# GpSimd's store of one output group: three transfers become eight, with other shares for the DMA engines

## The chip, the core and the metric

The kernel runs on one core of a Trainium2 chip. The metric is the device time of one execution in microseconds (us); of several executions the median counts. Three executions before the change took 516.02, 516.07 and 517.08 us, so the median is 516.07 us.

The core has five instruction queues: PE (TensorE), DVE (VectorE), ACT (ScalarE), POOL (GpSimd) and SP (SyncE), and sixteen DMA engines that carry every load and every store.

## The reference

The reference is a batched matrix product in float32, 128 products of a 256x512 by a 512x384 matrix:

```python
b1, b2, m, k, n = 8, 16, 256, 512, 384
x       # (8, 16, 256, 512) float32
weight  # (8, 16, 512, 384) float32
np.matmul(x, weight).astype(np.float32)
```

Every input is read once (64 MiB of `x`, 96 MiB of `weight`) and every output is written once (48 MiB).

## The kernel before

The 128 products are taken in `NG = 32` groups of `G = 4`. One group needs 2 MiB of `x` (tile `x_sb`, two buffers), 3 MiB of weights (`w_sb`, two buffers) and makes 1.5 MiB of output (`out_sb`, four slots of eight rows per partition). Input arrives as float32; DVE and ACT cast it to bfloat16 (`cast_x`, `cast_w`, `cast_short`), PE transposes `x` (`transpose`), ACT brings the transposes from PSUM to SBUF (`evacuate`), PE multiplies (`multiply`, for the last group `multiply_full`), and ACT copies the products from PSUM to `out_sb` (`copy_out`).

Every load and nearly every store is issued by SP in an order written out by hand (`on_sync`, line 312): the loads of the first four groups; then a loop over 26 groups that issues the load of `x` of group n+4, the store of group n and the load of the weights of group n+4; then the loads of groups 30 and 31, and at the end the stores of groups 27 to 31. The first four and the last two groups load their weights in two halves (`is_short`). The last group uses another layout (`is_full`): its load of `x` and its store move shorter runs.

One store is missing from SP's order: that of group 26, the sixth last (`SHARED = NG - 2 - LAG`, line 62). GpSimd issues it in `store_rest` (line 164), the only thing it does after building an identity matrix at the start. It waits until ACT has copied group 26 out and until the store of group 25 has landed. A store of a group covers 128 partitions with 12288 bytes each (eight rows of 384 float32). Before the change it goes in three transfers of 5, 120 and 3 partitions. An instruction that resets the cursor from which GpSimd's transfers are dealt to the DMA engines (`inc_swdge_sem` with `reset_dge_cursor`) stands ahead of the first and of the third. Each transfer adds 16 to `rest_out`.

`rest_out` is waited for in one place: ACT's `copy_out` (line 292) writes group 30 into the slot of `out_sb` that group 26 used, so ahead of its first copy of group 30 ACT waits for `16 * 3`.

At the end SP waits for the stores of groups 28 to 30 (`o_end`, line 329), runs sixteen increments of a semaphore that nobody reads (lines 330 to 333), and waits for the store of group 31 (`o_fin`, line 334), which ends the program.

Of the kernel before, what the change touches and what calls it, by code (L numbers as in the profile page):

```python
# [12 lines left out]
def kernel(  # L13
# [10 lines left out]
    _, _, _, N = weight.shape  # L24
# [18 lines left out]
    R = G * M // P  # L43
    T = R // 2
    SH, SL = 2, 4
    NG = B // G
# [5 lines left out]
    LAG = 4  # L52
# [6 lines left out]

    PAD = 12  # L60

    SHARED = NG - 2 - LAG

    ctx.enter_context(tc.tile_critical(sync_engine=mybir.EngineType.Pool, no_gpsimd_drain=True))  # L64

    def sbuf(name, shape, dtype, n):
        return [
            ctx.enter_context(nc.sbuf_tensor(f"{name}{s}", shape, dtype)) for s in range(n)
        ]
# [6 lines left out]
    def sems(name, n):  # L76
        return [tc.alloc_semaphore(f"{name}{s}") for s in range(n)]
# [9 lines left out]
    out_sb = sbuf("out_sb", [P, OS * R, N], fp32, 1)[0]  # L87
# [16 lines left out]
    rest_out = sems("rest_out", 1)[0]  # L104
# [59 lines left out]
    def store_rest(e):  # L164
        n = SHARED
        e.wait_ge(o_copied, n * T + T + BIAS)
        e.wait_ge(o_out[(n - 1) % 2], 16 + 16 * ((n + 1) // 2))
        dram = o_rows[n * G * M : (n + 1) * G * M].rearrange("(p r) n -> p r n", r=R)
        a = slot(0, NG, n) * R
        p = 0  # L170
        for k, reset in ((5, True), (120, False), (3, True)):
            if reset:
                e.inc_swdge_sem([], [], mode="reset_dge_cursor")
            e.dma_start(  # L174
                out=dram[p : p + k],
                in_=out_sb[p : p + k, a : a + R],
                max_dma_last_dim=R // 2 * N * 4,
            ).then_inc(rest_out, 16)
            p += k

    def is_shared(n):
        return isinstance(n, int) and n == SHARED

    def slot(t, U, s):
        return (t * U + s) % OS
# [106 lines left out]
    def copy_out(e, t, U, s, q):  # L292
        n = t * U + s
        if q == 0:
            if isinstance(n, int) and is_shared(n - OS):
                e.wait_ge(rest_out, 16 * 3)
            elif not isinstance(n, int) or n >= OS:
                e.wait_ge(o_out[s % 2], (t * (U // 2) + s // 2) * 16 + (16 - OS // 2 * 16 + 16))
        e.wait_ge(p_made, n * T + (q + 1 + BIAS))
        e.copy(  # L300
            out=out_sb[:, bass.ds(slot(t, U, s) * R + 2 * q, 2), :],
            in_=po[(s * T + q) % PO][:, :, :N],
        ).then_inc(o_copied, 1)

    def on_gpsimd(e):
        e.memset(identity[:], 0.0).then_inc(id_done, 1)  # L306
        e.wait_ge(id_done, 1)
        make_identity(nc, identity[:], nomemset=True)
        e.drain().then_inc(id_done, 1)
        store_rest(e)  # L310
# [70 lines left out]
    def on_scalar(e):  # L381
# [8 lines left out]
        def step(t, U, s):  # L390
            short = is_short(t * U + s + 1)
            evacuate(e, t, U, s + 1, range(T - 1))
            for q in range(T):
                copy_out(e, t, U, s, q)
                if q == 0:
                    evacuate(e, t, U, s + 1, range(T - 1, T))
                if q == 0 and short:
                    e.sem_inc(w_acast, CA)
                if q > 0 and not short:
                    last = CA if q == T - 1 else q  # L400
                    cast_w(e, t, U, s + 1, range(CV + q - 1, CV + last), q == 1)
# [11 lines left out]
        for q in range(T):  # L413
            copy_out(e, 0, NG, NG - 1, q)
# [36 lines left out]
```

## Time and profile before

| | |
|---|---|
| median of three executions | 516.07 us |
| the profiled execution's own time | 515.93 us |
| its span in the profile | 514.2 us |
| read and written in HBM | 167.77 MB and 50.33 MB |
| mean rate over the span | 424 GB/s |
| DVE and ACT busy | 397.6 us (77%) and 409.6 us (80%) |
| PE busy | 312.7 us (61%) |
| POOL busy | 3.8 us (1%) |
| granted TensorE clock, mean | 0.792 |

The profile shows one execution. Its first part gives the busy time of each engine, its second the span in 40 equal slices, its third the DMA queues, where q1 is what SP issues and q0 what GpSimd issues. The fourth part follows the chain of work that ended last, the fifth lists the costliest groups of instructions, the sixth the DMA issues with the time from issue to landing. "Busy" for the DMA engines is the time that their packets took, as a share of sixteen engines. The trace behind the profile also holds each DMA packet with its queue, its size, its start and its length, though not the number of the engine that moved it.

### The profile page before, as it was taken

How to read it: one execution, taken by the hardware profiler on the slowest of the kernel's cores; microseconds unless marked ns; L12 is line 12 of the kernel's file. 1: busy time of each engine (PE TensorE's matmuls, PEld its weight loads, DVE VectorE, ACT ScalarE, POOL GpSimd, SP SyncE). 2: the span in 40 equal slices, each digit the busy share in tenths (PEclk: the TensorE clock that was granted, in tenths of full speed). 3: DMA queues.
4: the chain of work that ended last, by engine and by line, in shares of the span. 5: the costliest groups of instructions: out<-in, count | busy, mean ns of one | idle time of the engine just before them, and what ended most of it. 6: DMA issues, size and time to landing. Idle time of an engine off the chain costs nothing.

```text
span 514.2 us, 11663 instructions
## 1 busy us (share of the span) xinstructions
PE 312.7 (61%) x4512; PEld 220.0 (43%) x4512; DVE 397.6 (77%) x462; ACT 409.6 (80%) x387; POOL 3.8 (1%) x9
## 2 busy tenths in 40 slices
PE   2276737546575656865666754577547576655872
PEld 2254425434354443543444543445434354442551
DVE  2788757797777887778977779777798777887980
ACT  1365577897987997898989799879897987998662
POOL 0000000000000000000000000000000000010000
PEclk9698878777876887686778687878777886878697
DMA  8999999999999999999999999999999999999997
GB/s 335 430 427 422 441 422 425 432 431 437 428 422 434 432 431 435 423 428 433 437 429 433 422 434 434 431 432 422 433 437 434 429 427 429 431 436 421 422 429 306
DMA packets 15686, 218.18 MB, mean 424 GB/s; under 512 B 1728, under 2 KB 1728, under 8 KB 3008
## 3 DMA queue, kind: packets, MB, share of 16 engines
q1 hardware_dynamic: 15312, 216.54, 98.8%
q0 software_dynamic: 368, 1.57, 0.7%
q8 instruction: 3, 0.05, 0.0%
q14 instruction: 3, 0.02, 0.0%
HBM read 167.77 MB, written 50.33 MB: 424 GB/s over the span
## 4 chain that ended last, share of the span: by engine, by line
DMA 55%; DVE 31%; issue 9%; PE 1%; DVEq 1%; SPq 1%; ACT 0%; POOLq 0%
DMA w_sb<-in_weight_dram 55%; DVE w_bf L207 20%; DVE w_bf L223 5%; DVE x_bf L194 5%; PE po L283 1%; SPq L138 0%; DVEq L358 0%; SPq L121 0%; DVEq L64 0%; DVEq L203 0%; ACT out_sb L300 0%; SPq L133 0%; DVEq L191 0%; DVEq L217 0%; SPq L446 0%
## 5 line engine op out<-in xcount | busy, mean ns | idle before, releaser
L207 DVE CAST w_bf<-w_sb 32x1536 bf16<-32x1536 f32 x286 | 271.9, 951 | 81.7 <-DMA w_sb<-in_weight_dram 70.5
L265 PE MATMUL po<-w_bf,x_t 128*32 128x384 bf16 x3968 | 194.6, 355 | 35.2 <-DVE w_bf L207 23.3
L247 PE MATMUL pt<-identity,x_bf 128*128 128x128 f32 x512 | 113.1, 409 | 155.2 <-DVE x_bf L194 155.2
L207 ACT CAST w_bf<-w_sb 32x1536 bf16<-32x1536 f32 x130 | 190.9, 1468 | 5.1 <-DMA w_sb<-in_weight_dram 2.0
L247 PEld LDWEIGHTS pt<-identity,x_bf 128*128 128x128 f32 x512 | 101.6, 223 | 167.5 <-issue 167.0
L265 PEld LDWEIGHTS po<-w_bf,x_t 128*32 128x32 bf16 x3968 | 115.4, 104 | 112.9 <-issue 50.0
L300 ACT COPY out_sb<-po 128x768 f32 (+1 forms) x128 | 102.4, 800 | 59.3 <-PE po L265 54.1
L234 ACT COPY x_t<-pt 128x1024 bf16<-128x1024 bf16 x128 | 123.5, 1020 | 20.6 <-PE pt L247 20.0
L194 DVE CAST x_bf<-x_sb 128x1024 bf16<-128x1024 f32 x128 | 80.0, 688 | 12.4 <-DMA x_sb<-in_x_dram 11.6
L223 DVE CAST w_bf<-w_sb 64x1536 bf16<-64x1536 f32 x48 | 45.8, 955 | 7.3 <-DMA w_sb<-in_weight_dram 6.0
L234 ACT ACT_TABLE_LOAD x1 | 1.3, 1283 | 10.8 <-PE pt L247 10.8
L174 POOL DMA_DIRECT2D out_dram<-out_sb x3 | 3.1, 1040 | 458.7 <-DMA out_dram<-out_sb 458.7
L283 PE MATMUL po<-w_bf,x_t 128*128 128x384 bf16 x32 | 5.4, 326 | 1.6 <-DVE w_bf L223 1.6
L283 PEld LDWEIGHTS po<-w_bf,x_t 128*128 128x128 bf16 x32 | 3.1, 98 | 3.9 <-issue 1.9
masks.py:199 POOL TENSOR_SCALAR_AFFINE_SELECT identity<-identity 128x128 f32<-128x128 f32 x1 | 0.3, 284 | 0.2 <-POOL identity L306 0.2
L306 POOL MEMSET identity<- 128x128 f32 x1 | 0.2, 205 | 0.5 <-POOLq L64 0.5
L435 POOL MEMSET const-bfloat16-1.0<- 128x1 bf16 x1 | 0.1, 97 | 0.0
L435 POOL MEMSET const-uint8-127<- 128x1 uint8 x1 | 0.1, 97 | 0.0
L435 POOL MEMSET const-float32-0.0<- 128x1 f32 x1 | 0.1, 93 | 0.3 <-issue 0.3
L435 POOL MEMSET const-float32-1.0<- 128x1 f32 x1 | 0.1, 93 | 0.0
## 6 DMA issues: line engine op xcount, KB each, us to landing
w_sb<-in_weight_dram SPq DMA_DIRECT2D x26, 3072.0 KB, 18.1
x_sb<-in_x_dram SPq DMA_DIRECT2D x32, 2048.0 KB, 22.2
out_dram<-out_sb SPq DMA_DIRECT2D x31, 1536.0 KB, 24.9
w_sb<-in_weight_dram SPq DMA_DIRECT2D x12, 1536.0 KB, 16.7
out_dram<-out_sb POOLq DMA_DIRECT2D x1, 1440.0 KB, 17.0
out_dram<-out_sb POOLq DMA_DIRECT2D x1, 60.0 KB, 7.3
out_dram<-out_sb POOLq DMA_DIRECT2D x1, 36.0 KB, 17.9
```

The costliest lines, as they stand in the source:

```text
L174: e.dma_start(out=dram[p : p + k], in_=out_sb[p : p + k, a : a + R], max_dma_last_dim=R // 2 * N * 4,).then_inc(rest_out, 16)
L194: e.tensor_copy(out=x_bf[s % BS][:, rows].rearrange("p r (s q c) -> p r s q c", s=S, c=KO), in_=x_sb[s % XS][:, rows].rearrange("p r (q s ...
L207: copy(out=w_bf[(s * G + i) % WBS][h * C : (h + 1) * C], in_=w_sb[s % WS][i * C : (i + 1) * C, h * KO : (h + 1) * KO, :],).then_inc(w_vcas ...
L223: e.tensor_copy(out=w_bf[(n * G + d * SH + a) % WBS][h * p : (h + 1) * p], in_=w_sb[n % WS][a * p : (a + 1) * p, r : r + KO, :],).then_inc ...
L234: e.copy(out=x_t[s % TS][:, 2 * q : 2 * q + 2], in_=pt[(s * T + q) % PT][:].bitcast(bf16),).then_inc(t_copied, 1)
L247: ins = e.transpose(pt[(s * T + q) % PT][:, rr, h, :], words[:, 2 * q + rr, h :: KO // 2], identity[:],)
L265: ins = e.matmul(po[(s * T + q) % PO][mine, rr, :N], x_t[s % TS][:, 2 * q + rr, ko // 2, mine, ko % 2], w_bf[(s * G + i) % WBS][:, ko, :], ...
L283: ins = e.matmul(po[(s * T + q) % PO][:, rr, :N], x_t[s % TS][:, 2 * q + rr, ko // 2, :, ko % 2], w_bf[(s * G + q) % WBS][:, ko, :], start ...
L300: e.copy(out=out_sb[:, bass.ds(slot(t, U, s) * R + 2 * q, 2), :], in_=po[(s * T + q) % PO][:, :, :N],).then_inc(o_copied, 1)
L306: e.memset(identity[:], 0.0).then_inc(id_done, 1)
L435: nc = _bacc.Bacc("TRN2", target_bir_lowering=False, num_devices=1)
```

## The change

`store_rest` sends group 26 in eight transfers instead of three. The list gives for each whether the cursor is reset ahead of it, its first partition, the count of partitions, and which of the eight rows of each partition it takes (`lo` to `hi`). The first five partitions go in two halves of four rows, as transfers one and four. The rest goes whole, in transfers of 3, 72, 40, 2, 4 and 2 partitions. The cursor is reset four times. The longest run of one descriptor, `max_dma_last_dim`, stays half of what a partition sends in that transfer: 6144 bytes, and 3072 in the two half transfers. ACT waits for `16 * 8` in place of `16 * 3`. Bytes, source, destination and the waits ahead of the store are as before, and nothing else in the program differs.

```diff
-    SHARED = NG - 2 - LAG
+    SHARED, PARTS = NG - 2 - LAG, 8
...
-        p = 0
-        for k, reset in ((5, True), (120, False), (3, True)):
+        H = R // 2
+        parts = [
+            (True, 0, 5, 0, H),
+            (False, 5, 3, 0, R),
+            (False, 8, 72, 0, R),
+            (True, 0, 5, H, R),
+            (False, 80, 40, 0, R),
+            (False, 120, 2, 0, R),
+            (True, 122, 4, 0, R),
+            (True, 126, 2, 0, R),
+        ]
+        assert len(parts) == PARTS
+        for reset, p, k, lo, hi in parts:
             if reset:
                 e.inc_swdge_sem([], [], mode="reset_dge_cursor")
             e.dma_start(
-                out=dram[p : p + k],
-                in_=out_sb[p : p + k, a : a + R],
-                max_dma_last_dim=R // 2 * N * 4,
+                out=dram[p : p + k, lo:hi],
+                in_=out_sb[p : p + k, a + lo : a + hi],
+                max_dma_last_dim=(hi - lo) // 2 * N * 4,
             ).then_inc(rest_out, 16)
-            p += k
...
             if isinstance(n, int) and is_shared(n - OS):
-                e.wait_ge(rest_out, 16 * 3)
+                e.wait_ge(rest_out, 16 * PARTS)
```

## The prediction, made before the changed kernel ran

> **What bounds the kernel now.** The head of the page first, then its DMA queues and the chain that ended last.
>
> ```profile
> span 514.2 us, 11663 instructions
> ...
> DMA  8999999999999999999999999999999999999997
> DMA packets 15686, 218.18 MB, mean 424 GB/s; under 512 B 1728, under 2 KB 1728, under 8 KB 3008
> ...
> q1 hardware_dynamic: 15312, 216.54, 98.8%
> q0 software_dynamic: 368, 1.57, 0.7%
> q8 instruction: 3, 0.05, 0.0%
> q14 instruction: 3, 0.02, 0.0%
> ...
> DMA 55%; DVE 31%; issue 9%; PE 1%; DVEq 1%; SPq 1%; ACT 0%; POOLq 0%
> ```
>
> The sixteen DMA engines are full from the first slice to the last but one: 98.8% + 0.7% of their time. No byte is saved by this change, so only the ends can give time: engines that stop early while others still work. The windows of the last 7 us show that. The two columns that matter stand at the end of each row, DMA share and GB/s.
>
> ```profile
> 505.50:506.00 0.50, 0.00 (x0) 0.00 (x0) 0.00 (x0) 0.00 (x0) 0.00 (x0) 1.00 0.86 369
> 506.00:506.50 0.50, 0.00 (x0) 0.00 (x0) 0.00 (x0) 0.00 (x0) 0.00 (x0) 1.00 0.70 295
> 506.50:510.00 3.50, 0.00 (x0) 0.00 (x0) 0.00 (x0) 0.00 (x0) 0.00 (x0) 0.79 1.01 406
> 510.00:510.40 0.40, 0.00 (x0) 0.00 (x0) 0.00 (x0) 0.00 (x0) 0.00 (x0) 0.50 1.01 399
> 510.40:511.00 0.60, 0.00 (x0) 0.00 (x0) 0.00 (x0) 0.00 (x0) 0.00 (x0) 0.50 0.50 200
> 511.00:511.50 0.50, 0.00 (x0) 0.00 (x0) 0.00 (x0) 0.00 (x0) 0.00 (x0) 0.50 0.31 123
> 511.50:512.00 0.50, 0.00 (x0) 0.00 (x0) 0.00 (x0) 0.00 (x0) 0.00 (x0) 0.50 0.27 102
> 512.00:512.50 0.50, 0.00 (x0) 0.00 (x0) 0.00 (x0) 0.00 (x0) 0.00 (x0) 0.50 0.06 25
> ...
> SPq L330 <- DMA out_dram<-out_sb: 3.0, 1, 3.0
> SPq L333 <- DMA out_dram<-out_sb: 1.3, 1, 1.3
> ```
>
> At 510.4 half of the engines are done; four or five work on to 512.0. What is done after 510.4 is 0.6 x 0.50 + 0.5 x (0.31 + 0.27 + 0.06) = 0.62 us of all sixteen. Spread evenly it would end at 511.0 instead of about 512.3: **1.3 us is the most that levelling can give**, and the dip to 0.70 ahead of 506.5, engines that wait for the last store, adds at most 0.2 us. SP waits for the stores to the end (3.0 and 1.3 us), so the last landing sets the time. Arithmetic is not behind it:
>
> ```profile
> 481.78 24.11 SPq L160 DMA_DIRECT2D out_dram<-out_sb  x5
> ...
> 499.28 5.37 PE po L283 x32
> ...
> 504.67 0.80 ACT out_sb L300
> ```
>
> The last store is issued at 505.5, as soon as ACT has copied; by the packet records early engines start it at 506.44 and end it at 510.4, late ones take it up when the stores ahead of it are done.
>
> **Who is late.** No view names the DMA engine of a packet, but the trace's packet records can be strung together: each packet begins some 4 ns before the recorded end of the one before it on its engine, and every engine moves the same list of SP's packets. That gives sixteen strings. Lag below is how far an engine ends a store behind the earliest engine (us), after the store of group 25 (just ahead of GpSimd's) and of group 30; "full" counts 6144-byte packets of q0. Strings are named by the start of their first packet (ns).
>
> ```
> first packet  1949 1955 1977 1998 2008 2056 2122 2209 2376 2469 2664 2775 2789 2942 2981 3418
> lag, group 25 0.00 1.12 1.24 0.93 0.20 0.13 0.62 3.56 0.25 0.47 0.67 0.48 2.50 2.49 2.60 0.91
> full packets    16   18   20   20   16   16   16    2   20   16   16   16   16   16   16   16
> lag, group 30 0.00 1.59 2.14 1.84 0.19 0.13 0.63 1.48 1.16 0.48 0.66 0.47 2.54 2.50 2.62 0.90
> ```
>
> So GpSimd's store is already a lever: one engine gets one partition (two packets) and falls from last to the middle; two partitions more cost 0.91 us (1.84 - 0.93), or 0.455 each. The row of q0 in the stretch in which it runs agrees: 23.7% of 16 engines x 16 us over 128 partitions is 0.474.
>
> ```profile
> q0 software_dynamic: 365, 1.57, 23.7%
> ...
> out_dram<-out_sb POOLq DMA_DIRECT2D x1, 1440.0 KB, 17.0
> out_dram<-out_sb POOLq DMA_DIRECT2D x1, 60.0 KB, 7.3
> out_dram<-out_sb POOLq DMA_DIRECT2D x1, 36.0 KB, 17.9
> ```
>
> Three engines remain 2.5 to 2.6 late. Early in the run each lost about a microsecond to one of q8's three packets (instructions), at 15.2, 39.3 and 46.0 us; these are the rows of q8 in three windows of 0.5 us, from 15.0, 39.0 and 45.8 (13% of sixteen engines x 0.5 us is 1.04 us of one engine):
>
> ```profile
> q8 instruction: 1, 0.02, 12.9%
> ...
> q8 instruction: 1, 0.02, 13.8%
> ...
> q8 instruction: 1, 0.02, 13.6%
> ```
>
> **How the parts are dealt.** q0's 368 packets are 16 x (3 + 17 + 3): in each transfer every engine gets as many entries as a carrying engine (two per partition, plus one for the semaphore), idle ones as 4-byte fillers. So 5 partitions went to five engines, 120 to fifteen by eights, 3 to three; 120 began behind the five, and skipped the fifth. I count places from the cursor's reset. By the same dealing the new list gives: halves, places 0 to 4; 3 to places 5 to 7; 72 on twelve by sixes, 8 to 15 and 0 to 3; after a reset, the other halves on 0 to 4; 40 on ten by fours, 5 to 14; 2 to places 15 and 0; 4 to 0 to 3; 2 to 0 and 1. Partitions by place, before and after:
>
> ```
> place    0  1  2  3  4  5  6  7  8-14  15
> before  10 10 10  9  1  8  8  8     8   8
> after   10  9  8  8  1  5  5  5    10   7
> ```
>
> The strings with 20, 18 and 2 full packets are places 0 to 2, 3 and 4. The other eleven, three of them late, are places 5 to 15 in an order that the trace doesn't tell outright.
>
> The Trainium skill, DMA: Bandwidth & Descriptors, section "Why a DMA increments its semaphore by 16 and not by 1", has the count of engines as the largest number up to 16 that divides the partitions, but names an exception on this path with sixteen engines and partitions / 16 rounded up. The 368 packets fit the first; whether 72 and 40 keep to it no row shows. By the exception the sum would be that of rival three.
>
> **The sum.** If the late three hold places 5 to 7, each gives up three partitions: 2.62 - 1.37 = 1.25. Seven of the eight early ones take two more: 0.66 becomes 1.57, and 0.90 becomes 1.81, or 0.44 if that one is place 15. Places 0 to 2 keep 2.14 at worst (if the engine with 2.14 is place 0), 1.39 at best (1.84 loses one partition, 2.14 loses two: 1.23). Place 3: 1.13; place 4 stays at 1.48. The worst lag is thus 1.57 to 2.14 instead of 2.62: a gain of 1.05 down to 0.48. I take the upper end, because the string with 0.90 began last of all, which points to place 15, and only one order in three leaves 2.14 where it is.
>
> Costs. Entries per engine go from 23 to 16-fold (3+3+13+3+9+3+3+3) = 640 packets, 40 each. Seventeen more of 9 ns, half of it overlapped: 0.08 us for each engine, on the path. POOL's issues:
>
> ```profile
> 460.46 3.12 POOL L174 DMA_DIRECT2D out_dram<-out_sb  x3 [458.75 <-DMA out_dram<-out_sb]
> ...
> 493.66 0.80 ACT L300 COPY out_sb<-po 128x768 f32<-128x768 f32 x1 [0.39 <-PE po L265]
> ```
>
> Eight instead of three at 1.04 us is 8.3 us, to 468.8; nothing is queued behind them on POOL, so nothing is paid. The resets pay at most as much as an issue, and have the same cover. The wait for `16 * 8`: the old store had landed by 480.5 (the last issue at 462.6 plus 17.9). One turn of q0 per engine took (480.5 - 465) / 23 = 0.67 us, as q1's packet goes in between; forty turns end by 492 at most, sooner where group 31's short load packets alternate. ACT's first copy of group 30 stands at 493.66, and what is queued behind it is the rest of group 30 and then 31. The cover is 1.7 us or more; if it were gone, ACT's delay would have to pass the slack of the last store, 506.44 against the late engines' 508.5, before it cost.
>
> So -1.05 + 0.08 = -0.97. The profiled execution took 515.93, its span 514.2 with 1.7 around it, and stands 0.14 under the median: 514.96 from the one, 515.10 from the other. I forecast **515.0 us**.
>
> **Rivals.** (1) The late three hold places 8 to 14. They then get two partitions more: 2.62 + 0.91 = 3.53, so +0.91 + 0.08, 517.1 us; slower. It decides as soon as one of them is there. For it: in order of first packets they are the 13th to 15th. Against it: that order puts the fifth place 8th, or 14th, since 2209 and 2942 end the first load in the same ns and may be swapped; with the second reading the fifth place stands right among the late three, as 5 to 7 would. (2) The lateness moves between executions: one of three took 1.0 us longer (517.08), the size of one q8 packet. Then gains and losses mix, about 516.0. Against it: the other two executions and the profiled one lie within 0.14. (3) 72 and 40 are dealt over all engines, by fives and threes: the fifth place gets 9 instead of 1, 1.48 + 8 x 0.455 = 5.1, +2.5, 518.6 us. (4) The lateness that is levelled is refilled, for example since the last store can't start before 506.44 or instructions are fetched late by other engines: half the gain at most, 515.6.
>
> **Numbers.** No change is within 0.2%, 1.03 us, or 515.04 to 517.10, about what measurement can tell. The forecast has 0.60 and straddles that line (514.8 to 515.6): 0.38 faster, 0.22 no change. Rival 1 has 0.20 (0.14 slower, 0.06 none), rival 2 0.07 (0.02, 0.02, 0.03 slower), rival 3 0.08, all slower, rival 4 0.05, none. Faster 0.40, same 0.35, slower 0.25. The range, 514.6 to 517.1, holds all but rival 3 and the far half of rival 1; its low end is the profiled 515.93 less the 1.3 of full levelling.
>
> **What would show it.** Dealing: q0 with 640 packets and 1.57 MB, 1990 packets under 512 B. Places: in the last windows the DMA share stays near 1 to about 511 and is gone by 511.5; if rival 1 holds, three engines work on to 513.2 (a share near 0.19); if rival 3, one engine alone to 515. Span 513.2. The waits on POOL and ACT: eight issues from 460.5 to 469, ACT's copy of group 30 at 493.7, still released by PE. A share that falls at 510.4 as before would mean that the last 2 us have another cause than the dealing.

## The result, and the profile after

The changed kernel takes **517.32 us** (median of 11 executions, 517.19 to 517.50) where the kernel before takes 515.95 in the same comparison (515.68 to 517.08): a ratio of 1.0026, with a 95% interval of 1.0018 to 1.0033. It is 1.37 us slower, where 1 us faster was forecast. The head of the page of the changed kernel, its DMA queues, GpSimd's group of issues, and the size and landing time of those transfers:

```profile
span 515.5 us, 11670 instructions
...
DMA packets 15926, 218.19 MB, mean 423 GB/s; under 512 B 1968, under 2 KB 1968, under 8 KB 3248
...
q1 hardware_dynamic: 15312, 216.54, 98.6%
q0 software_dynamic: 608, 1.57, 0.8%
...
L185 POOL DMA_DIRECT2D out_dram<-out_sb x8 | 6.4, 805 | 458.8 <-DMA out_dram<-out_sb 458.8
...
out_dram<-out_sb POOLq DMA_DIRECT2D x1, 864.0 KB, 13.9
out_dram<-out_sb POOLq DMA_DIRECT2D x1, 480.0 KB, 15.7
out_dram<-out_sb POOLq DMA_DIRECT2D x2, 30.0 KB, 10.4
```

The bytes are the same, and the span grew by 1.3 us. q0's 608 packets are 16 x 38. The windows of the last 8 us of the changed kernel (DMA share and GB/s at the end of each row):

```profile
506.00:506.50 0.50, 0.00 (x0) 0.00 (x0) 0.00 (x0) 0.00 (x0) 0.00 (x0) 1.00 0.63 270
506.50:510.00 3.50, 0.00 (x0) 0.00 (x0) 0.00 (x0) 0.00 (x0) 0.00 (x0) 0.61 0.96 387
510.00:510.40 0.40, 0.00 (x0) 0.00 (x0) 0.00 (x0) 0.00 (x0) 0.00 (x0) 0.50 1.03 407
510.40:511.00 0.60, 0.00 (x0) 0.00 (x0) 0.00 (x0) 0.00 (x0) 0.00 (x0) 0.50 0.83 328
511.00:511.50 0.50, 0.00 (x0) 0.00 (x0) 0.00 (x0) 0.00 (x0) 0.00 (x0) 0.50 0.26 104
511.50:512.00 0.50, 0.00 (x0) 0.00 (x0) 0.00 (x0) 0.00 (x0) 0.00 (x0) 0.50 0.18 74
512.00:512.50 0.50, 0.00 (x0) 0.00 (x0) 0.00 (x0) 0.00 (x0) 0.00 (x0) 0.50 0.20 80
512.50:513.00 0.50, 0.00 (x0) 0.00 (x0) 0.00 (x0) 0.00 (x0) 0.00 (x0) 0.50 0.21 84
513.00:513.50 0.50, 0.00 (x0) 0.00 (x0) 0.00 (x0) 0.00 (x0) 0.00 (x0) 0.50 0.02 6
```

From 511.5 to 513.0 the share stands at 0.18 to 0.21. One engine of sixteen is 0.0625, so three engines work alone for 1.5 us: the mark that the first rival had set for itself. By the trace's semaphore records the last store lands at 513.57, where it landed at 512.69 before: +0.88. The other 0.4 us lies behind the landing, a stretch that the prediction had left out. These are the drains of GpSimd's sequencer in the block that ends the program, by their line (least / median / greatest ns), before and after:

```profile
L446 POOLq DRAIN  x3: 34/108/313, 513.0 to 513.9; - x3
```

```profile
L456 POOLq DRAIN  x3: 34/108/722, 513.9 to 515.2; - x3
```

The longest one comes first, right after SP's last wait, and the program ends behind it: 0.722 - 0.313 = 0.41 us. 0.88 + 0.41 is the 1.3 us of the span.

The packet records of the changed kernel, strung together as for the prediction, and ordered by their full packets (one more string with twenty, which is place 0, and those of places 1 to 3 are left out; none of them is late):

```
full packets  lag after store 25 -> lag after store 30
20, places 8-14   2.24 -> 3.95   2.42 -> 4.15   2.51 -> 4.21   (the late three)
20, places 8-14   0.16 -> 1.84   0.23 -> 1.93   0.30 -> 1.98   0.71 -> 2.39
10, places 5-7    0.00 -> 0.06   0.06 -> 0.15   0.53 -> 0.00
14, place 15      0.82 -> 1.13
 2, place 4       3.54 -> 2.18
```

The three engines with ten packets, which gave up three partitions each, were early ones; the late three have twenty. They end their last store at 512.87 to 513.07, where the late three of the kernel before ended theirs at 512.12 to 512.24. (Lag counts from the earliest engine. That is now one of those that gave up partitions, so all the others read some 0.8 us more than in the table before.)

### The profile page after: what moved, and what is told of

Read it like the earlier page. It is cut to its first block, busy times and chain, and to the rows that moved or that the text cites. A ratio compares the mean times of both kernels' runs of the same rounds, so it can differ in the third digit from the quotient of the medians.

```text
span 515.5 us, 11670 instructions
## 1 busy us (share of the span) xinstructions
PE 311.7 (60%) x4512; PEld 220.8 (43%) x4512; DVE 397.7 (77%) x462; ACT 409.6 (79%) x387; POOL 7.1 (1%) x14
## 4 chain that ended last, share of the span: by engine, by line
DMA 55%; DVE 31%; issue 9%; PE 2%; SPq 0%; DVEq 0%; ACT 0%; POOLq 0%
DMA w_sb<-in_weight_dram 55%; DVE w_bf L217 22%; DVE x_bf L204 5%; DVE w_bf L233 3%; PE po L293 1%; PE po L275 1%; SPq L138 0%; DVEq L201 0%; DVEq L64 0%; ACT out_sb L310 0%; SPq L133 0%; SPq L121 0%; DVEq L227 0%; SPq L456 0%; POOLq L64 0%
## 5 line engine op out<-in xcount | busy, mean ns | idle before, releaser
L185 POOL DMA_DIRECT2D out_dram<-out_sb x8 | 6.4, 805 | 458.8 <-DMA out_dram<-out_sb 458.8
```

What stands on the lines that cost most here:

```text
L185: e.dma_start(out=dram[p : p + k, lo:hi], in_=out_sb[p : p + k, a + lo : a + hi], max_dma_last_dim=(hi - lo) // 2 * N * 4,).then_inc(rest_ ...
```

## The experiments

The times of the kernel before beside these runs were 515.91 (e1 to e4), 515.85 (e5 to e8), 515.80 (e9 to e11, one execution), 515.95 (e12), 516.00 (e13, e14) and 515.96 (e15, e16). Each kernel starts from the changed one, unless it says otherwise; only the list of transfers is shown (reset, first partition, partitions, first and last row), and the limit on a run where it differs.

**Which places are late (e1).** Fifteen transfers of 15, 14, ... 2 and at last 9 partitions, each after a reset, so that each place has its own number of packets.

```diff
+            (True, 0, 15, 0, R),
+            (True, 15, 14, 0, R),
+            (True, 29, 13, 0, R),
...
+            (True, 117, 2, 0, R),
+            (True, 119, 9, 0, R),
```

> The share of each place is made different, so that each DMA engine's string of packets tells its place: fifteen transfers of 15, 14, ... 2 and 9 partitions, a reset ahead of each, give places 0 to 15 the counts 15, 15, 14, 13, 12, 11, 10, 9, 8, 6, 5, 4, 3, 2, 1, 0. Theory (the three engines that lose a microsecond to q8's instruction packets hold places 8 to 14, and the time went to their two further partitions): all three strings with a q8 packet show counts from 8 down to 1. Rival (they sit elsewhere, or move from run to run, and the time went into the number of transfers): one of them at least shows 9 or more, or 0. The time itself is no test here; POOL's last DRAIN, if it goes with the number of transfers, is 0.31 + 12 x 0.082 = 1.3 us.

521.53 us in one execution. The strings that are 2.89, 2.31 and 2.27 late after store 25 carry six, four and two full packets, thus three, two and one partition: **places 12, 13 and 14**. The slow engine, 3.64 late, has the 24 packets of place 4. So the first rival's condition holds in this execution, and holds for all three; the changed kernel's own strings, with twenty packets on each of its late three, agree. The end of GpSimd's drain also followed the number of transfers, 15 here:

```profile
L463 POOLq DRAIN  x3: 34/107/1293, 517.2 to 519.1; - x3
```

**The number of transfers, apart from the shares (e2, e5).** Eight transfers, but the shares of before. The 120 partitions go in two halves of four rows. In e2 the limit on a run of memory is 6144 bytes, so that each such half is one run; in e5 it stays at 3072 bytes, so that each half has two runs by the instruction (in both traces a half moves as one packet of 6144 bytes).

```diff
             (True, 0, 5, 0, H),
+            (False, 5, 120, 0, H),
             (True, 0, 5, H, R),
+            (False, 5, 120, H, R),
+            (True, 125, 3, 0, 2),
+            (True, 125, 3, 2, 4),
+            (True, 125, 3, 4, 6),
+            (True, 125, 3, 6, 8),
...
-                max_dma_last_dim=(hi - lo) // 2 * N * 4,
+                max_dma_last_dim=min(hi - lo, H) * N * 4,
```

The last two lines are e2's alone.

> Eight transfers as in the changed kernel, but every place gets the partitions that it had before (10, 10, 10, 9, 1, then 8). Theory (0.9 us of the 1.3 us in the spans are the two further partitions on the late engines, 0.4 us is POOL's last DRAIN, which grows by 0.08 us with each transfer): +0.4 to +0.5 us over the kernel before, DRAIN near 0.72 us, last landing as before near 512.7. Rival A (the number of transfers is the whole price): +1.3 us. Rival B (the shares are the whole price): 0.

> The second experiment again, now with two runs of a descriptor per partition, as the change has them, so that the 120 partitions go to fifteen engines behind the first five and the slow engine of place 4 gets one partition, as before the change. Eight transfers, old shares. Theory (0.9 us of shares on the late engines, 0.4 us of POOL's last DRAIN): last landing as before (512.7), DRAIN 0.72 us, +0.4 to +0.5 us over the kernel before. Rival A (the number of transfers is the whole price): +1.3 us. Rival B (shares alone): 0.

e2 missed what it was made for: 518.93 us (518.87 to 519.05), a ratio of 1.0059 [1.0045, 1.0073]. Its last windows show one engine alone (a share of 0.06) from 512.0 on; its packets end near 514.5:

```profile
511.50:512.00 0.50, 0.00 (x0) 0.00 (x0) 0.00 (x0) 0.00 (x0) 0.00 (x0) 0.50 0.29 111
512.00:512.50 0.50, 0.00 (x0) 0.00 (x0) 0.00 (x0) 0.00 (x0) 0.00 (x0) 0.50 0.06 25
...
513.00:513.50 0.50, 0.00 (x0) 0.00 (x0) 0.00 (x0) 0.00 (x0) 0.00 (x0) 0.50 0.06 25
```

By the strings it is the slow engine: the 120 partitions were dealt by eights over places 0 to 14, both times, and gave place 4 nine partitions instead of one; the engine of place 15 got none. The last store lands at 515.23 instead of 512.69: +2.5, the price that the third rival had put on such a dealing. Nearly all the rest of e2's +3.0 us is GpSimd's drain (714 ns instead of 313). With two runs in each partition (e5) the same 120 began behind the five and skipped place 4, as in the kernel before. The Trainium skill, DMA: Bandwidth & Descriptors, section "Why a DMA increments its semaphore by 16 and not by 1", knows both ways of dealing: the largest divisor up to 16, and for some direct copies sixteen engines with partitions / 16 rounded up, from engine 0. e2 looks like the second (120 / 16 rounded up is 8), the others like the first; here the number of runs in a partition decided which, since the limit on a run is all in which e2 and e5 differ.

e5: 516.29 us (516.02 to 516.82), +0.44 against 515.85, a ratio of 1.0008 [0.9999, 1.0017], with the old shares confirmed by the strings, the last landing at 512.87 (512.69 before) and this drain:

```profile
L456 POOLq DRAIN  x3: 34/107/722, 513.2 to 514.5; - x3
```

By the times alone +0.44 is not clear of noise; the drain's part of it stands in the trace, 0.722 - 0.313 = 0.41. Between the two profiled spans the five transfers more cost 0.6 us: the drain, and 0.18 on the landing.

**The drain taken out of the end (e3, e4).** The changed kernel (e3) and the kernel before (e4), with GpSimd draining as soon as its store has landed, 30 us ahead of the end:

```diff
         store_rest(e)
+        e.wait_ge(rest_out, 16 * PARTS)
+        e.drain()
```

> The changed kernel, with GpSimd waiting for its own store and draining at once, some 20 us ahead of the end, where it has nothing else to do. Theory (POOL's last DRAIN retires the transfers and is on the path after the last landing): the last DRAIN falls from 0.72 to 0.1 us or so, the time by 0.5 to 0.6 us against the changed kernel, to +0.8 us over the kernel before. Rival (the DRAIN is long for another reason, as the last landing): the last DRAIN stays near 0.72 us and the time with it.

> The kernel before, with the same early drain after its three transfers. Theory: the last DRAIN falls from 0.31 to 0.1 us or so, and the time by 0.2 us, which would make it the fastest so far. Rival: no change in either.

```profile
L322 POOLq DRAIN  x1: 722/722/722, 484.2 to 484.2; - x1
...
L458 POOLq DRAIN  x3: 34/34/108, 514.0 to 514.6; - x3
```

Those are e3's drains: the 722 ns are now at 484.2, and the last drains take 34 to 108 ns. e3: 516.65 us (516.38 to 517.13), ratio 1.0016 [1.0007, 1.0025], 0.67 less than the changed kernel. e4: 515.75 (515.56 to 515.87), ratio 0.9996 [0.9987, 1.0005], 0.16 less than the kernel beside it. With the drain out of both, the shares make 516.65 - 515.75 = 0.90 us (with whatever else eight transfers cost besides the drain, which e5 leaves small). So the 1.37 us fall into 0.90 for the shares (e3 against e4) and 0.44 for the number of transfers (e5 against before): 1.34.

**Fewer partitions where the lateness is (e6, e7, e8).** The idea of the change with the places that e1 found. e6 gives places 12 to 14 five partitions, 0 to 3 ten, 4 one and the others nine; e7 gives 12 to 14 four, 5 to 11 ten, 0 to 3 nine, 15 eight and 4 one (the last partition is spread over all engines, with a shorter limit on its run); both with the early drain. e8 is e7 without it.

```diff
             (True, 0, 5, 0, H),
-            (False, 5, 3, 0, R),
-            (False, 8, 72, 0, R),
+            (False, 5, 45, 0, R),
             (True, 0, 5, H, R),
-            (False, 80, 40, 0, R),
-            (False, 120, 2, 0, R),
-            (True, 122, 4, 0, R),
-            (True, 126, 2, 0, R),
+            (False, 50, 49, 0, R),
+            (False, 99, 3, 0, R),
+            (False, 102, 25, 0, R),
+            (False, 127, 1, 0, R),
...
-                max_dma_last_dim=(hi - lo) // 2 * N * 4,
+                max_dma_last_dim=(hi - lo) // (2 if k > 1 else R) * N * 4,
```

That is e7; e6 has 60, then 35, 3 and 25, and the old limit.

> Places 12 to 14, where the staircase run found the three late engines, get five partitions; places 0 to 3 ten, 4 one, 5 to 11 and 15 nine; six transfers, early drain. Theory: the late engines fall below 1.5, and the largest lag after the store of group 30 becomes that of places 1 and 3 (about 2.0, two engines that each lost a microsecond to an instruction packet of q14 and now have ten), instead of 2.6: -0.55 us, and -0.2 us for the DRAIN: 515.1 to 515.2 us where the kernel before takes 515.9. Rival (the shares of this store don't reach the end, and the changed kernel lost its time to something else): no faster than the kernel before with the early drain, 515.75.

> Shares cut to the lags that the staircase run shows: places 12 to 14 four, 5 to 11 ten, 0 to 3 nine, 4 one, 15 eight, and one partition spread over all sixteen; seven transfers, early drain. Theory: the largest lag after the store of group 30 is 1.5 to 1.7 instead of 2.6, -0.9 us, and -0.2 us for the DRAIN: 514.8 us. Rival (as in the run before): 515.75.

> The same shares and transfers without the early drain. Theory: last DRAIN 0.31 + 4 x 0.082 = 0.64 us, last landing as in the run before, so 0.6 us slower than that one: 515.4 us. Rival (the DRAIN is no part of the path): as the run before.

The profiled executions of e6 and e7 came out as worked out, within 0.2: 515.31 and 514.90 us. e8's, 515.84, is 0.4 above what was expected: its drain took 640 ns as worked out, but its last store landed 0.41 later than e7's (512.26 against 511.85). e7's last windows have no tail left:

```profile
510.40:511.00 0.60, 0.00 (x0) 0.00 (x0) 0.00 (x0) 0.00 (x0) 0.00 (x0) 0.50 0.49 195
511.00:511.50 0.50, 0.00 (x0) 0.00 (x0) 0.00 (x0) 0.00 (x0) 0.00 (x0) 0.50 0.15 59
511.50:512.00 0.50, 0.00 (x0) 0.00 (x0) 0.00 (x0) 0.00 (x0) 0.00 (x0) 0.50 0.00 0
```

The medians did not: 515.87 (515.31 to 516.31), 516.39 (514.88 to 516.76) and 516.91 (515.84 to 517.63), ratios of 1.0000 [0.9991, 1.0009], 1.0002 [0.9993, 1.0011] and 1.0021 [1.0012, 1.0030]. e7 has two groups of times: four executions from 514.88 to 515.11, seven from 516.38 to 516.76, and nothing between. The changed kernel has no such groups, nor has the kernel before, which was above 516.5 in one execution only (517.08). (Where the times fall into two groups, the ratio given is not that of the medians: e7's median lies 0.54 above the 515.85 beside it, at a ratio of 1.0002.)

**What makes the second group (e9 to e16).** e9, e10 and e11 are e7 again, to catch a profile of the upper group.

> The same kernel as e7_late_four_rest_nine_ten, looked at again, to catch an execution of its second group of times (516.4 to 516.8 against 514.9 to 515.1). Theory: lateness is not the same in every execution (the second of the rivals), so in an execution near 516.4 the largest lag of an engine at store 30 is about 1.5 us above the 1.64 of the first profile, at a place that the first profile had level, and the last landing is near 513.35 where it was 511.85. Rival a: the landing stays within 0.3 us of 511.85 and the 1.5 us lie behind it, in the last DRAIN. Rival b: the whole chain before the last store (ACT's copies of group 30) is later by 1.5 us, and the lags are as they were.

> A third look at the same kernel. By the theory a time near 514.9 goes with a last landing near 511.85 and a time near 516.4 with one near 513.35 and a largest lag near 3.1 us; by rival a the landing is the same in both, by rival b the issue of the last store is later by the difference.

> A fourth look at the same kernel, with the expectations of the third: theory, time 516.4 with a largest lag near 3.1 us at store 30; rival a, the same landing with a longer end; rival b, a later last store with the same lags.

They took 515.22, 515.22 and 515.25 us, all near the lower group, so they told nothing of the upper one. In the profiles of e7, e9 and e10 the late three lie in places 12 to 14; e11 took the same time.

e12 gives all of places 10 to 15 six partitions, e13 all of 8 to 14 seven (and place 4 four), e14 gives places 5 to 10 five.

```diff
             (True, 0, 5, 0, H),
+            (False, 5, 75, 0, R),
             (True, 0, 5, H, R),
+            (False, 80, 10, 0, R),
+            (False, 90, 27, 0, R),
+            (False, 117, 11, 0, R),
```

That is e13; e12 has 75, then 25 and 6, four times 4 after a reset, and 1; e14 has 45, then 6, 63, 8 and 1.

> Places 0 to 3 get ten partitions, 4 one, 5 to 9 ten, and all of 10 to 15 six (one partition is spread over all), with the early drain. Theory: the late three do not hold places 12 to 14 in every execution but a neighbouring three in most (11 to 13 or 13 to 15), and that made the second group of e7_late_four_rest_nine_ten: an engine that is 2.5 late and has ten partitions where it was to have four ends 6 x 0.455 = 2.7 later, 1.1 to 1.5 past the worst place of the good executions. With six places low the worst place is the same in both cases, 2.9 + 6 x 0.455 = 5.6 against 1.08 + 10 x 0.455 = 5.6 for place 3, so nearly all executions lie at 515.3 to 515.6, in one group. Rival a: the late three move further than 10 to 15; then there are still two groups, the upper one 1.0 to 1.8 higher. Rival b: the 1.5 us has nothing to do with the places; then the upper group is again 1.5 above the lower one, in most executions.

> Partitions by place: 10 10 10 9 4, then 9 9 9 on 5 to 7, 7 on each of 8 to 14, 9 on 15; six transfers, the early drain. Theory: the late three lie somewhere within places 8 to 14 in every execution (the changed kernel, which gave all of these ten, was slow in all eleven), at 12 to 14 in only some, so that with seven on each of them all executions end alike: 2.8 + 7 x 0.455 = 6.0 for a late engine, 1.1 + 10 x 0.455 = 5.6 for places 0 to 3; against 515.46 in the profile of e12_last_six_low, whose worst was 5.7 with four transfers more, 515.6, in one group no wider than 0.5. Rival (the second group has nothing to do with the places): again some executions at 515.6 and others 1.0 to 1.5 above.

> Partitions by place: 11 11 11 11 2, then 5 on each of 5 to 10, 11 on 11, 10 on 12 to 15; seven transfers, the early drain. The profile, with the late three on 12 to 14: 2.8 + 10 x 0.455 = 7.35 where the worst of e7_late_four_rest_nine_ten had 5.3, so 514.9 + 2.0 = 516.9. Theory: in some of the timed executions the late three lie lower, and where all are within 5 to 10 the worst is 1.1 + 11 x 0.455 = 6.1: one to three of ten executions near 515.8, the others at 516.9 to 517.4. Rival (the places are the same in every execution, and the second group of the other kernels is something that is added): all at 516.9, or some at 516.9 and others above it by 1.0 to 1.5, none below 516.6.

e12: 515.55 us (515.25 to 516.83), ratio 0.9999 [0.9990, 1.0008]; seven of eleven executions at 515.25 to 515.69, three at 516.43 to 516.83, one at 516.01. That is not the one group that was expected; its upper group lies 1.0 to 1.4 above the lower, as its rival a has it, by which the late three move further than places 10 to 15. e13: 516.28 (515.99 to 516.53), ratio 1.0005 [0.9996, 1.0014], one group. It lies 0.7 above what was expected, which has another cause than the late three; its last windows show one engine alone:

```profile
511.50:512.00 0.50, 0.00 (x0) 0.00 (x0) 0.00 (x0) 0.00 (x0) 0.00 (x0) 0.50 0.14 55
512.00:512.50 0.50, 0.00 (x0) 0.00 (x0) 0.00 (x0) 0.00 (x0) 0.00 (x0) 0.50 0.07 29
512.50:513.00 0.50, 0.00 (x0) 0.00 (x0) 0.00 (x0) 0.00 (x0) 0.00 (x0) 0.50 0.00 0
```

That is the slow engine of place 4, which loses a further 0.3 to 0.4 us while SP's last stores run (its lag goes from 2.65 after store 27 to 2.94 after store 30 in e13, and from 3.06 to 3.46 in e16, the same kernel; it is the largest lag in both, the next are 2.40 and 2.71). Four partitions were one or two too many for it. e14: 516.74 (515.61 to 517.03), ratio 1.0013 [1.0004, 1.0022]; ten executions at 516.47 to 517.03, and one at 515.61, 1.1 below the profiled execution (516.74), which fits no execution with three engines as late in places 12 to 14. As e13 and e7 had run on different chips, both ran again on one:

> The kernel of e7_late_four_rest_nine_ten again, timed on one chip together with that of e13_seven_places_at_seven, since the two had run on different chips. Theory: the late three change place within 8 to 14 from execution to execution on any chip; again two groups, near 515 and near 516.5, at least a fifth of the executions in each, a spread of 1.5 or more. Rival (the chip of e7 was the unsteady one): one group, within 0.6 us.

> The kernel of e13_seven_places_at_seven again, beside e15_late_four_beside_e16 on the same chip. Theory: one group, 515.9 to 516.6, whatever the other kernel does. Rival (what made the second group of e7 is something added, whatever the shares): a spread like that of the kernel beside it.

e15: four executions at 514.85 to 515.29, seven at 516.23 to 516.79, ratio 1.0004 [0.9995, 1.0013]. e16: one group, 515.98 to 516.75 (a spread of 0.77, a little more than expected), ratio 1.0006 [0.9997, 1.0015]. On the same chip, then, the kernel that relieves places 12 to 14 alone has two groups 1.5 us apart, and the one that relieves 8 to 14 alike has one. That speaks for engines whose lateness differs from one execution to the next, and against 1.5 us that is added at the end whatever the shares. It doesn't tell where they are: e16's slow engine of place 4, 0.75 behind the late three, hides most of what a late engine would lose in places 5 to 7 or 15 (two partitions more than in 8 to 14, 0.91), and it could also hide part of what a further engine lost that became late besides the three. And nothing of this is seen directly: no profile caught an execution of the upper group, and why the profiled executions (e7, e8, e9, e10, e11 and e15, all with e7's shares) were all of the lower one stays open.

## Why the prediction was wrong

- **The step that failed** is the first sentence of the sum: "If the late three hold places 5 to 7". They hold 12 to 14 in the profiled executions (e1), so the engines that gave up three partitions were early, and the late ones took two more. The order of first packets had pointed there ("they are the 13th to 15th"). It was put second because another reading, in which two strings that end the first load in the same ns change places, set the fifth place among the late three. One swap that could be made or not was no evidence for places 5 to 7; the three that stood next to each other at the end were some for 12 to 14.
- **The first rival's size was right.** It gave +0.91 for two partitions at 0.455 each and a share near 0.19 to 513.2. Measured: +0.88 on the last landing, +0.90 between e4 and e3, a share of 0.18 to 0.21 to 513.0. Its +0.99 with the entries fell 0.38 short of the measured +1.37, because of the next point; its time of 517.1 is only 0.2 short, as it started from 516.07, the median of three executions, and not from 515.95.
- **GpSimd was costed at nothing.** That "nothing is queued behind them on POOL, so nothing is paid" was wrong: the drain that ends the program is queued there, and waits for nothing but itself. It takes 313 ns with 3 transfers, 558 with 6, 640 with 7, 722 with 8 (714 in e2), 885 with 10 and 1293 with 15: 82 ns more for each. It follows neither the packets (722 ns with q0's 608 packets, and in e5 with 480) nor the resets (four, and in e5 six). Five more cost 0.41 us on the path, five times what was put down for the entries (0.08).
- **The entries** came to 38 for each engine instead of 40: the halves of five partitions moved as one packet of 6144 bytes each, where two had been counted. e5's landing, 0.18 later with 30 entries instead of 23, bounds this term, and e3 less e4 (0.90 against 0.91 for the partitions alone) leaves it near nothing.
- **The dealing** was right: the largest divisor up to 16, twelve for 72 and ten for 40, from where the cursor stood; as many strings have 20, 18, 16, 14, 10 and 2 full packets as the list of places says. Rival three's case did not come up, but e2 gave place 4 its nine partitions by another way, and the landing came the 2.5 later that the rival had worked out.
- **GpSimd's issues and ACT's wait** were covered, as said. These are GpSimd's issues and ACT's first copy of group 30 in the changed kernel's timeline:

```profile
460.51 6.41 POOL L185 DMA_DIRECT2D out_dram<-out_sb  x8 [458.80 <-DMA out_dram<-out_sb]
...
494.85 0.80 ACT L310 COPY out_sb<-po 128x768 f32<-128x768 f32 x1 [1.59 <-PE po L275]
```

The eight issues take 6.4 us, where 8.3 was the estimate, and end at 466.9; ACT is released by PE, not by the eight landings. The copy is 1.2 us later than before, and the last store's issue 0.4 (505.93 against 505.50). The dip at 506 grew a little, to 0.63, yet the late three take up the last store only at 509.1 to 509.4, when the stores ahead of it are done, so it set nothing.

- **Lateness that moves between executions** (the second rival, 0.07) did not show in this change: all eleven executions lie within 0.31. Places 8 to 14 all got ten, so it made no difference which of them were late. It is the likely cause of the spread in e6 to e8 instead, which is argued and not seen.

## What to carry to other kernels

Before work is dealt away from late engines, find out which they are by a run that gives each a number of its own, as the fifteen transfers of e1 did; an order read from start times is a guess. Levelling to one execution's lags pays only if the same engines are late in every execution: compare the spread of times, not the profiled one alone. And count what an issue leaves behind at the very end of its own engine: a drain that lengthens with every transfer can be moved under other work by waiting for those transfers and draining early.

No version here beats the kernel before by more than these runs can tell: e12, at 515.55 against 515.95, and e4, at 515.75 against 515.91, come nearest.

## What the runs showed of the hardware

- GpSimd's drain at the end of the program takes 82 ns more for each transfer that it has issued and not drained, though all had landed some 30 us earlier; the cost is paid once, wherever the first drain after them stands (e3).
- With one run of memory per partition a transfer of 120 partitions was dealt from place 0, with two runs from where the cursor stood (e2 and e5).
- A transfer of one partition, with a limit of 1536 bytes on a run, went out as sixteen pieces of 768 bytes, one for each engine (e7: 2034 packets under 2 KB, but 2018 under 512 B):

```profile
DMA packets 15990, 218.19 MB, mean 425 GB/s; under 512 B 2018, under 2 KB 2034, under 8 KB 3312
```
